# Filling the standing operands of a five-phase product stage: raw halves loaded into the places of their own low parts, instead of through two spare buffers

## The chip, the cores and the metric

One core of one Trainium2 chip runs the kernel. The metric is device microseconds of one execution. The kernel before took 1764.42 us (median of 3 runs, 1763.62 to 1765.13). The profiled execution, from which every duration below comes, took 1766.1 us, of which 1763.9 us lie between its first and its last instruction.

## The reference

One layer of a decoder trunk, in float32, for 2048 positions of width 1024:

```
mod = silu(c) @ w_ada + b_ada;  shift, scale, gate = split(mod, 3)
u = x * (1 + scale) + shift
q, k, v, a_gate, p_in, p_gate, m_a, m_p = split(u @ w_in)
a = sliding_window_sink_attention(q, k, v, sinks, bias, mask) * silu(a_gate)
a = a @ w_attn_proj
p = grouped_linear(multiscale_causal_pool(p_in)) * pool_scale * silu(p_gate)
p = p @ w_pool_proj
y = (sigmoid(m_a) * a + sigmoid(m_p) * p) @ w_out * (1 + gate)
x = layer_norm(2**0.25 * x + y)
```

The change touches the stage of the last three products: `a @ w_attn_proj`, `p @ w_pool_proj` and `y @ w_out`.

## The kernel before

**Products in parts.** A float32 matrix product is done as three products of the rounded type fp32r: every operand is split into a high part (a cast, on ACT) and a low part (operand minus high part, a tensor_tensor on DVE), and `mm3` multiplies high by high, high by low and low by high. Besides, products of 2 x 2 blocks are done with seven block products in place of eight (`front`, `back`), so that for one half of the sequence the standing operand is kept as seven blocks, named B11, T1, T2, B21, T3, B22 and T4. The profile leaves the numbers of names out: its `set_B` is B11, B21 or B22, and its `set_T` is T1 to T4. One *set* is a tile of 128 x 4 x 2 x 512: four pieces of 512 columns, each with a high and a low place beside each other. One *product* below is `product(...)`: one set against one split weight, 4 pieces x 3 = 12 matmuls.

**The last stage** runs in five phases of products: attention projection of sequence half 0, pool projection of half 0, the same two for half 1, and the output projection. The sets are the same tiles in all phases, so between two phases all seven are filled anew. Each phase has groups of two quads (a quad is a 2 x 2 block of the weight), and one group takes 14 products in a fixed order, which the prediction numbers 0 to 13: T2 and B21 of the first quad (0, 1), T2 and B21 of the second (2, 3), T3 and B22 of the first (4, 5), T3 and B22 of the second (6, 7), T4 twice (8, 9), and then, for the next group, B11 and T1 of its first quad (10, 11) and of its second (12, 13). After each product `tick` calls what hooks are due at that position. In the last group of a phase, products 10 to 13 and all that follow need the sets of the next phase; I call the last group of a phase with the first products of the next a *hand-over*. There are four. In three of them (attention to pool, pool to attention, attention to pool) the new sets lie in DRAM unsplit, as two halves of 512 KB each, and `set_steps` loads and splits them; for the fourth (pool to output) they lie there split already and are loaded straight into place by `fill_set`, which the change does not touch.

**What `set_steps` does before.** It takes the 14 halves in the order of PLAN. The raw half goes into a *spare* buffer (`ph.spare()`, 128 x 1024; this pool has two); at its position in SPLIT_AT a cast on ACT writes the high places (profile: `ACT CAST set_B<-spare`, or `set_T`), and a subtraction on DVE the low places (`DVE TENSOR_TENSOR set_B<-spare,set_B`). The first two halves are asked for at position 0, and half k + 2 at the position of the split of half k, whose buffer it takes over.

**What sets the order.** Each engine runs its own queue in order. `sp` issues nearly all loads and stores of this stage, so a load on it waits behind whatever the queue waits for. The other users of the queues in a hand-over are these:

- The weights: `Quad.load` loads a quad into W (two buffers) and A22; POOL forms sums (L294, `sum1`; L298 and L299, `mid`; L303, `late`); `pair_split` casts on ACT (L325) and subtracts on DVE (L132); `half_split` does the same for T4 (L332, L132). PE's products wait for these.
- The gates: each quad gives four results of two halves, and for each of the eight results of a group a 256 KB piece of the gate is loaded (`ga`, L587, in attention phases; `gp`, L597, in pool phases). DVE multiplies the result by it (L590, L598).
- In pool phases POOL adds the gated result to the attention part (L600, `wide`), and `sp` stores the sum three ticks later (`y_d<-wide`, 256 KB).
- DVE also adds partial products in PSUM (L383, L405), and ACT copies them there (L368, L369).

Of the kernel before, what the change touches and what calls it, by code (L numbers as in the profile page):

```python
# [59 lines left out]
def kernel(  # L60
# [23 lines left out]
    pe, act, dve, pool, sp = (Ordered(tc, e) for e in (nc.tensor, nc.scalar, nc.vector, nc.gpsimd, nc.sync))  # L84
# [6 lines left out]
    def set_tile(pl, n):  # L91
        return pl.tile([P, 4, 2, CH], F32R, tag=f"set_{n}", name=f"set_{n}")

    sets = {n: set_tile(cp, n) for n in ("B11", "T1", "B21")}
# [33 lines left out]
    def as32(ap):  # L128
        return ap.bitcast(F32)

    def low(engine, dst, src, hi):
        engine.tensor_tensor(dst, src, as32(hi), ALU.subtract)  # L132
# [53 lines left out]
    def split_set(name, i, src, n=1, eng=None):  # L186
        a, d = eng or (nc.scalar, nc.vector)
        t = sets[name]
        dst = t[:, i : i + n]
        hi, lo = dst[:, :, 0, :], dst[:, :, 1, :]  # L190
        if n == 1:
            hi, lo = t[:, i, 0, :], t[:, i, 1, :]
        a.copy(hi, src)
        low(d, lo, src, hi)
# [6 lines left out]
    def fill_set(name, half, src, eng=None):  # L201

        dst = as32(sets[name][:, 2 * half : 2 * half + 2])
        (eng or nc.sync).dma_start(dst, src[2 * half : 2 * half + 2].rearrange("i p h c -> p i h c"))
# [115 lines left out]
    def by_two(t):  # L320
        return t.rearrange("p (a c) -> p a c", a=2)
# [175 lines left out]
    def steps(hooks, groups, start, todo):  # L497
# [9 lines left out]
    PLAN = (  # L507
        (0, "B11", 0), (1, "B11", 1), (2, "T1", 0), (4, "T1", 1), (5, "T2", 0), (6, "T2", 1), (8, "B21", 0),
        (9, "B21", 1), (11, "T3", 0), (12, "T3", 1), (14, "B22", 0), (15, "B22", 1), (17, "T4", 0), (18, "T4", 1),
    )  # L510

    SPLIT_AT = (1, 2, 3, 4, 6, 7, 11, 12, 13, 14, 15, 16, 17, 18)

    def set_steps(ph, store):


        if store["B11"].shape[0] == 4:
            return [(p, lambda n=n, h=h: fill_set(n, h, store[n])) for p, n, h in PLAN]
        raw, todo = {}, []

        def fetch(k):
            name, half = PLAN[k][1:]
            raw[k] = ph.spare()
            sp.dma_start(raw[k], store[name][half].rearrange("p a b -> p (a b)"))

        def split(k):
            name, half = PLAN[k][1:]
            split_set(name, 2 * half, by_two(raw[k]), 2, (act, dve))

        for k, at in enumerate(SPLIT_AT):  # L530
            if k < 2:
                todo.append((0, lambda k=k: fetch(k)))
            todo.append((at, lambda k=k: split(k)))
            if k + 2 < len(SPLIT_AT):
                todo.append((at, lambda k=k: fetch(k + 2)))
        return todo

    def planned(hooks, ph, store, last, pending={}):
        if last:
            pending["steps"] = set_steps(ph, store)  # L540
        for p, f in pending["steps"]:
            if (p < 14) == last:
                hooks.setdefault((-1, p) if last else (0, p - 14), []).append(f)
        return hooks
# [967 lines left out]
```

## Time and profile before

| | us |
|---|---|
| median of 3 runs | 1764.42 |
| profiled execution | 1766.1 |
| its span, first to last instruction | 1763.9 |
| PE busy (share of the span) | 1702.4 (97%) |
| DVE busy | 1206.9 (68%) |
| ACT busy | 934.1 (53%) |
| POOL busy | 794.2 (45%) |

The five phases of products take the span from about 1283 us to its end. The hand-overs that the change touches begin with their product 0 at 1323.67 (attention to pool, half 0), 1399.83 (pool to attention) and 1511.40 us (attention to pool, half 1). A busy share is an average over the whole span, so the prediction goes by stretches of the span: for a stretch the profile gives the busy time of each engine, the granted clock of PE (1.00 is full) and the share of the DMA engines. A row of waits gives the waiting engine and line, what it waited for, the total in us, how many times, and the longest. A row of a timeline gives start and length in us, the engine, the line, the operation and, in brackets, the idle time ahead of it with what ended it.

### The profile page before, as it was taken

How to read it: one execution, taken by the hardware profiler on the slowest of the kernel's cores; microseconds unless marked ns; L12 is line 12 of the kernel's file. 1: busy time of each engine (PE TensorE's matmuls, PEld its weight loads, DVE VectorE, ACT ScalarE, POOL GpSimd, SP SyncE). 2: the span in 40 equal slices, each digit the busy share in tenths (PEclk: the TensorE clock that was granted, in tenths of full speed). 3: DMA queues.
4: the chain of work that ended last, by engine and by line, in shares of the span. 5: the costliest groups of instructions: out<-in, count | busy, mean ns of one | idle time of the engine just before them, and what ended most of it. 6: DMA issues, size and time to landing. Idle time of an engine off the chain costs nothing. (4 is left out here: it accounts for less than half of the span.)

```text
span 1763.9 us, 24990 instructions
## 1 busy us (share of the span) xinstructions
PE 1702.4 (97%) x8248; PEld 1427.4 (81%) x8248; DVE 1206.9 (68%) x2178; ACT 934.1 (53%) x1973; POOL 794.2 (45%) x618
## 2 busy tenths in 40 slices
PE   6899999999999998999999999999999989999997
PEld 5688888878888887888788888888888867888785
DVE  5977665655777776766655367777867676764777
ACT  4644444545777775544444377777734343423452
POOL 2154444431356567534434125456763562364542
PEclk9999999999999999999999999999999999999998
DMA  9385767844354567787777634544796675789442
GB/s 364 117 289 174 269 208 270 273 145 132 108 174 147 171 217 288 249 288 253 258 264 261 232 96 135 177 159 141 265 349 215 197 256 169 240 302 386 162 143 108
DMA packets 180466, 381.30 MB, mean 216 GB/s; under 512 B 18785, under 2 KB 39281, under 8 KB 180337
## 3 DMA queue, kind: packets, MB, share of 16 engines
q1 hardware_dynamic: 173696, 363.92, 60.5%
q0 software_dynamic: 3552, 11.56, 1.7%
q10 hardware_dynamic: 3088, 4.23, 0.8%
q8 instruction: 65, 1.06, 0.3%
q14 instruction: 65, 0.52, 0.1%
HBM read 244.35 MB, written 138.44 MB: 217 GB/s over the span
## 5 line engine op out<-in xcount | busy, mean ns | idle before, releaser
L56 PE MATMUL mm<-set_B,w_set 128*128 128x512 f32 x3240 | 798.7, 395 | 14.5 <-ACT u L376 6.3
L56 PEld LDWEIGHTS mm<-set_B,w_set 128*128 128x128 f32 x3240 | 603.3, 189 | 142.6 <-DVE w_set L132 10.3
L56 PE MATMUL lg<-set_T,w_set 128*128 128x512 f32 x2088 | 509.1, 394 | 18.4 <-DVE w_set L132 11.0
L56 PEld LDWEIGHTS lg<-set_T,w_set 128*128 128x128 f32 x2088 | 391.4, 189 | 111.0 <-DVE w_set L132 17.9
L132 DVE TENSOR_TENSOR w_set<-W,w_set 128x1024 fp32r<-128x1024 f32 x162 | 227.9, 1407 | 185.8 <-ACT w_set L325 180.8
L325 ACT CAST w_set<-W 128x1024 fp32r<-128x1024 f32 x162 | 169.8, 1049 | 251.6 <-PE mm L56 190.3
L56 PE MATMUL mm<-set_T,w_set 128*128 128x512 f32 x1080 | 265.5, 394 | 0.0
L56 PEld LDWEIGHTS mm<-set_T,w_set 128*128 128x128 f32 x1080 | 200.5, 188 | 41.0
L294 POOL TENSOR_TENSOR W<-W,A 128x512 f32<-128x512 f32 x56 | 82.1, 1466 | 227.6 <-DMA W<-in_win_dram 63.6
L303 POOL TENSOR_TENSOR W<-W 128x512 f32<-128x512 f32 x56 | 80.5, 1438 | 174.5 <-DVE w_set L132 165.2
L56 DVE TENSOR_TENSOR o<-pv,o 64x128 f32<-64x128 f32 x256 | 72.3, 283 | 89.8 <-ACT o L56 86.9
L56 ACT ACTIVATE L<-L,nm 128x257 f32<-128x257 f32 (+1 forms) x256 | 127.1, 498 | 9.3 <-DVE nm L56 3.9
L298 POOL TENSOR_TENSOR W<-W 128x512 f32<-128x512 f32 x56 | 90.5, 1618 | 84.7 <-DVE w_set L132 75.6
L56 DVE CUSTOM_DVE_ANT_0 L<-lg,bt,nsink 128x256 f32<-128x256 f32 (+1 forms) x256 | 111.6, 473 | 5.0 <-PE lg L56 0.8
L299 POOL TENSOR_TENSOR W<-W 128x512 f32<-128x512 f32 x56 | 84.7, 1513 | 37.9 <-DMA W<-in_win_dram 21.9
L56 POOL TENSOR_TENSOR w_set<-W,w_set 128x1024 fp32r<-128x1024 f32 x14 | 33.7, 2404 | 139.6 <-ACT w_set L56 96.9
L56 POOL TENSOR_TENSOR p<-nxt,pg 128x512 f32<-128x512 f32 x32 | 41.7, 1302 | 105.5 <-DVE sm L56 101.8
L56 ACT COPY o<-pv 64x256 f32<-64x256 f32 x128 | 47.3, 370 | 78.0 <-PE pv L56 77.2
L56 DVE TENSOR_TENSOR ptl<-pt,pth 128x512 fp32r<-128x512 f32 (+1 forms) x128 | 85.7, 669 | 1.9 <-ACT pth L56 1.7
L56 PE MATMUL lg<-kk,qs 128*128 128x256 f32 (+1 forms) x512 | 80.5, 279 | 0.0
L56 ACT ACTIVATE L<-L,sm 128x256 f32<-128x256 f32 (+1 forms) x128 | 64.2, 502 | 29.8 <-DVE sm L56 29.8
L56 ACT CAST pth<-pt 128x512 fp32r<-128x512 f32 (+1 forms) x128 | 73.5, 574 | 10.3
(212 smaller groups left out, 2296.3 us busy)
## 6 DMA issues: line engine op xcount, KB each, us to landing
W<-in_win_dram SPq DMA_DIRECT2D x48, 512.0 KB, 5.5
w_set<-wmix_d SPq DMA_DIRECT2D x32, 512.0 KB, 5.4
W<-in_win_dram SPq DMA_DIRECT2D x34, 256.0 KB, 3.7
A<-in_win_dram SPq DMA_DIRECT2D x34, 256.0 KB, 5.1
ag_d<-sig SPq DMA_DIRECT2D x32, 256.0 KB, 3.8
pg_d<-sig SPq DMA_DIRECT2D x32, 256.0 KB, 4.0
ma_d<-sig SPq DMA_DIRECT2D x32, 256.0 KB, 4.0
mp_d<-sig SPq DMA_DIRECT2D x32, 256.0 KB, 4.0
```

The source lines that it names most:

```text
L56: return lambda *args, **kw: self.tc.keep_in_program_order(op(*args, **kw))
L132: engine.tensor_tensor(dst, src, as32(hi), ALU.subtract)
L294: e.tensor_tensor(self.w[:, 1, :], self.w[:, 2, :], self.a22, ALU.add)
L298: e.tensor_tensor(x[:, 1, :], x[:, 1, :], x[:, 0, :], ALU.subtract)
L299: e.tensor_tensor(x[:, 2, :], x[:, 0, :], x[:, 2, :], ALU.subtract)
L303: e.tensor_tensor(x[:, 3, :], x[:, 3, :], x[:, 1, :], ALU.subtract)
L325: a.copy(by_two(hi), raw)
```

## The change

The spare buffers are no longer used here. A raw half (128 x 2 x 512) is loaded into the low places of the two pieces of the set that it will become, ACT casts from there into the high places, and DVE subtracts in place: low place minus high place, into the low place. A set can therefore be loaded only after its last product of the old phase. FETCH_AT names that position for each set, and both halves are asked for there: B11 and T1 at position 0, T2 at 3, B21 at 4, T3 at 7, B22 at 8, T4 at 10. The splits of B11 and T1 move one position later (2, 3, 4, 5 in place of 1, 2, 3, 4); the others keep theirs.

```diff
-    SPLIT_AT = (1, 2, 3, 4, 6, 7, 11, 12, 13, 14, 15, 16, 17, 18)
+    SPLIT_AT = (2, 3, 4, 5, 6, 7, 11, 12, 13, 14, 15, 16, 17, 18)
+
+    FETCH_AT = {"B11": 0, "T1": 0, "T2": 3, "B21": 4, "T3": 7, "B22": 8, "T4": 10}
...
-        raw, todo = {}, []
-
-        def fetch(k):
-            name, half = PLAN[k][1:]
-            raw[k] = ph.spare()
-            sp.dma_start(raw[k], store[name][half].rearrange("p a b -> p (a b)"))
-
-        def split(k):
-            name, half = PLAN[k][1:]
-            split_set(name, 2 * half, by_two(raw[k]), 2, (act, dve))
-
-        for k, at in enumerate(SPLIT_AT):
-            if k < 2:
-                todo.append((0, lambda k=k: fetch(k)))
-            todo.append((at, lambda k=k: split(k)))
-            if k + 2 < len(SPLIT_AT):
-                todo.append((at, lambda k=k: fetch(k + 2)))
-        return todo
+        todo = []
+
+        def raw(name, half):
+            return as32(sets[name][:, 2 * half : 2 * half + 2, 1, :])
+
+        def fetch(name, half):
+            sp.dma_start(raw(name, half), store[name][half])
+
+        def split(name, half):
+            t = sets[name][:, 2 * half : 2 * half + 2]
+            act.copy(t[:, :, 0, :], raw(name, half))
+            low(dve, t[:, :, 1, :], raw(name, half), t[:, :, 0, :])
+
+        for at, (_, name, half) in zip(SPLIT_AT, PLAN):
+            todo.append((FETCH_AT[name], lambda n=name, h=half: fetch(n, h)))
+            todo.append((at, lambda n=name, h=half: split(n, h)))
+        return sorted(todo, key=lambda t: t[0])
```

The first place where this moves instructions is SP's queue in the hand-over from pool to attention. `y_d` is the store of a result, `gp` a gate, `W` a weight; `ain1_B11` and the like are the raw sets in DRAM. Before, two raw halves stand together, and the next two only after them, between stores and weights:

```order
L56 DMA y_d_142<-wide3_13292 128x4x128
L56 DMA spare_13999<-ain1_B11_114 128x1024
L56 DMA spare_14001<-ain1_B11_114 128x1024
L597 DMA gp_14145<-mp_d_141 128x512
L56 DMA spare_14018<-ain1_T1_115 128x1024
L56 DMA spare_14047<-ain1_T1_115 128x1024
L597 DMA gp_14166<-mp_d_141 128x512
L287 DMA W_14091<-in_wap_dram 128x512
L289 DMA W_14091<-in_wap_dram 128x2x512
L56 DMA spare_14064<-ain1_T2_116 128x1024
L56 DMA spare_14088<-ain1_T2_116 128x1024
L56 DMA y_d_142<-wide4_13172 128x4x128
```

Now eight raw halves (B11, T1, T2, B21) stand ahead of the first weight:

```order
L56 DMA y_d_142<-wide3_13292 128x4x128
L598 DMA gp_14125<-mp_d_141 128x512
L56 DMA set_B11_66<-ain1_B11_114 128x2x512 x2
L56 DMA set_T1_67<-ain1_T1_115 128x2x512 x2
L56 DMA set_T2_235<-ain1_T2_116 128x2x512 x2
L56 DMA set_B21_68<-ain1_B21_117 128x2x512 x2
L56 DMA y_d_142<-wide4_13172 128x4x128
L287 DMA W_14071<-in_wap_dram 128x512
L289 DMA W_14071<-in_wap_dram 128x2x512
L56 DMA y_d_142<-wide6_13174 128x4x128
```

The weights of the next group moved behind the raw halves of T2 and B21, and the raw halves moved ahead of the stores that stood between them.

The second place is ACT's queue in the same hand-over, where PE waits for the casts of weights (L325). Before, the cast of the first half of B11 stands ahead of the cast of the second quad's weight (`W_13843`), and each cast of a set reads a spare buffer:

```order
L325 CAST w_set_13982<-W_13799 128x1024
L369 COPY p5_13978<-mm_13918 128x512
L56 CAST set_B11_66<-spare_13999 128x2x512
L368 COPY lg_14025<-mm_13951 128x512
L325 CAST w_set_14028<-W_13843 128x1024
L369 COPY p5_14024<-mm_13952 128x512
L56 CAST set_B11_66<-spare_14001 128x2x512
L325 CAST w_set_14070<-W_13799 128x1024
L56 CAST set_T1_67<-spare_14018 128x2x512
L56 CAST set_T1_67<-spare_14047 128x2x512
L325 CAST w_set_14117<-W_13843 128x1024
```

Now it stands behind it (the second quad's weight is `W_13829` here):

```order
L325 CAST w_set_13968<-W_13785 128x1024
L369 COPY p5_13964<-mm_13904 128x512
L368 COPY lg_14007<-mm_13937 128x512
L325 CAST w_set_14010<-W_13829 128x1024
L369 COPY p5_14006<-mm_13938 128x512
L56 CAST set_B11_66<-set_B11_66 128x2x512 x2
L325 CAST w_set_14050<-W_13785 128x1024
L56 CAST set_T1_67<-set_T1_67 128x2x512 x2
L325 CAST w_set_14099<-W_13829 128x1024
```

One cast of a set moved behind one cast of a weight; the later casts of sets keep their places among the weights.

## The prediction, made before the changed kernel had run

> **What bounds the kernel now.** I read the stretches of the span first, then the waits inside the stretch that loses time, then the timelines. Three stretches of 22 products each (the 14 of a hand-over and the next 8), from the start of product 0:
>
> ```profile
> 1323.67:1383.51 59.84, 59.84 (x266) 49.57 (x265) 47.80 (x48) 27.21 (x31) 22.44 (x14) 1.00 0.64 206
> 1399.83:1473.33 73.50, 64.53 (x266) 49.80 (x265) 56.04 (x48) 28.29 (x33) 36.77 (x22) 0.98 0.72 232
> 1511.40:1571.30 59.90, 59.90 (x265) 49.36 (x264) 41.19 (x38) 23.88 (x28) 33.80 (x21) 1.00 0.72 228
> ```
>
> The columns are length, then busy time of PE, its weight load, DVE, ACT and POOL, granted clock, DMA share, GB/s. The first and third, from attention to pool, run at 59.84 / 22 = 2.72 us a product with PE always busy: PE bounds them, and a faster split brings nothing there. The second, from pool to attention, does the same products in 73.50 us: 73.50 - 59.84 = 13.66 us are lost, and they are all that this change can win. Its waits:
>
> ```profile
> ACT set_T L56 <- DMA spare<-ain_T: 22.2, 8, 5.2
> ACT set_B L56 <- DMA spare<-ain_B: 18.3, 5, 7.3
> ...
> DVE w_set L132 <- ACT w_set L325: 10.5, 2, 8.8
> ...
> PE lg L56 <- DVE w_set L132: 5.6, 6, 1.9
> ...
> SPq L56 <- DVE set_B L56: 12.7, 5, 5.1
> SPq L56 <- POOL wide L600: 11.6, 6, 3.7
> SPq L56 <- DVE set_T L56: 6.4, 3, 2.7
> ```
>
> PE waits for split weights (L132), not for sets. But ACT stands 22.2 + 18.3 = 40.5 us before 13 casts whose raw half hasn't landed, and the casts of weights are queued behind them. SP asks late because it waits for the split that frees a spare buffer (12.7 + 6.4 us) and for POOL's sums (11.6), which its stores need. The chain reads so at the first stall, in the timelines of SP, ACT, DVE and PE:
>
> ```profile
> 1398.32 0.99 SPq L56 DMA_DIRECT2D spare<-ain_B  x2
> 1402.94 1.05 ACT L56 CAST set_B<-spare 128x1024 fp32r<-128x1024 f32 x1 [7.00 <-DMA spare<-ain_B]
> 1404.41 1.04 ACT L325 CAST w_set<-W 128x1024 fp32r<-128x1024 f32 x1
> 1405.49 1.23 DVE L132 TENSOR_TENSOR w_set<-W,w_set 128x1024 fp32r<-128x1024 f32 x1 [8.76 <-ACT w_set L325]
> 1406.77 2.56 PE L56 MATMUL lg<-set_T,w_set 128*128 128x512 f32 x10 [0.53 <-DVE w_set L132]
> ```
>
> The cast of the weight could have been made before 1402.94 but for the cast of B11 ahead of it. The loss by halves of the stretch, and DVE's part up to the first weight of product 14:
>
> ```profile
> 1399.83:1445.11 45.28, 39.99 (x169) 30.94 (x168) 35.28 (x29) 18.08 (x21) 28.89 (x16) 1.00 0.71 224
> 1445.11:1473.33 28.22, 24.54 (x98) 18.86 (x97) 20.75 (x20) 10.21 (x12) 7.88 (x6) 0.94 0.75 245
> 1405.49:1445.73 40.24, 35.01 (x146) 26.81 (x146) 35.90 (x29) 15.54 (x18) 28.36 (x15) 1.00 0.72 222
> ```
>
> Products 0 to 13 lose 45.28 - 14 x 2.72 = 7.20 us, products 14 to 21 lose 28.22 - 8 x 2.72 = 6.46 us.
>
> **The change part by part.** *The splits themselves* stay: 42 casts and 42 subtractions. A cast reading rows 1024 elements apart is already among L325's (the quad's second pair) and they do not differ; an in-place subtraction has a row too:
>
> ```profile
> L325 ACT CAST w_set<-W x47: 1038/1052/1057, 1289.7 to 1598.6; 128x1024 fp32r<-128x1024 f32 x47
> L132 DVE TENSOR_TENSOR w_set<-W,w_set x46: 1207/1226/2311, 1290.8 to 1596.7; 128x1024 fp32r<-128x1024 f32 x46
> L56 DVE TENSOR_TENSOR spare<-spare,cb x8: 1215/1767/2318, 715.7 to 932.3; 128x1024 f32<-128x1024 f32 x8
> ```
>
> 1215 against 1207 ns at the least: 0.01 us each, 0.3 us for 42, off PE's path; taken as nothing. *The loads* stay 512 KB but are written in pieces of 2 KB in place of 4. The nearest rows, weights in 2 KB pieces and ready sets of weights in 4 KB pieces:
>
> ```profile
> W<-in_win_dram SPq DMA_DIRECT2D x48, 512.0 KB, 5.5
> w_set<-wmix_d SPq DMA_DIRECT2D x32, 512.0 KB, 5.4
> ```
>
> 0.1 us of latency each; nothing, where a half is asked for 10 us ahead.
>
> *Earlier loads, pool to attention.* B11 still goes out behind the same store (1398.3), so its halves land at 1403 as now; but the cast of the second quad's weight now stands ahead of it, so the first stall goes. T1 waits for the end of its last product, 1399.83, and lands by about 1407 (raw halves here take 3.1 to 6.9 us, row below). T2 can go at the end of product 2 (1408.0) and is split at position 6, four products or 10.9 us later; B21 at the end of 3 for position 11; T3, B22 and T4 have 13 us and more. Before:
>
> ```profile
> 1412.34 1.05 ACT L56 CAST set_T<-spare 128x1024 fp32r<-128x1024 f32 x1 [4.51 <-DMA spare<-ain_T]
> 1422.22 1.05 ACT L56 CAST set_T<-spare 128x1024 fp32r<-128x1024 f32 x1 [5.17 <-DMA spare<-ain_T]
> 1448.27 1.05 ACT L56 CAST set_T<-spare 128x1024 fp32r<-128x1024 f32 x1 [4.42 <-DMA spare<-ain_T]
> 1466.62 4.15 PE L56 MATMUL lg<-set_T,w_set 128*128 128x512 f32 x10 [1.85 <-DVE w_set L132]
> ...
> DMA to landing us min/median/max: 3.1/4.4/6.9
> ```
>
> In products 14 to 21 POOL is nearly free and DVE has 28.22 - 20.75 = 7.5 us idle, nearly all behind such casts: I take the whole 6.46 us back there. In products 0 to 13 DVE itself comes next. From 1405.49 to 1445.73 it works 35.90 us; one subtraction (1.23) moves ahead, which leaves 34.7. It can begin at 1404.0, when the first raw half is cast, and ends no sooner than 1438.7. Product 14 would start at 1399.83 + 38.08 = 1437.9 and needs its low weight with its third matmul, at 1438.4. So 0.3 us is the least that stays lost, and 7.20 the most. DVE idles 40.24 - 35.90 = 4.3 us there now; half of it is its waiting for products, which stays: 2.2 us. With 0.5 us for restarts of PE I take 0.3 + 2.2 + 0.5 = 3.0 us as still lost. *Sum there: 13.66 - 3.0 = 10.7 us less*, between 6.5 and 13.4.
>
> *New waits, attention to pool.* SP now waits for PE: the next group's weights stand behind B21's load, thus behind the end of product 3. Now:
>
> ```profile
> 1331.94 0.33 SPq L287 DMA_DIRECT2D W<-in_wpp_dram  x1
> 1337.86 1.49 POOL L294 TENSOR_TENSOR W<-W,A 128x512 f32<-128x512 f32 x1 [10.50 <-DMA W<-in_wpp_dram]
> 1345.44 1.06 ACT L325 CAST w_set<-W 128x1024 fp32r<-128x1024 f32 x1 [1.80 <-issue]
> 1350.87 2.88 PE L56 MATMUL mm<-set_B,w_set 128*128 128x512 f32 x12
> ```
>
> Product 3 ends at 1323.67 + 4 x 2.72 = 1334.6; two loads later, at 1335.4, W goes, 3.5 us later than now. T2 and B21 (2 MB, from 1332 on) are ahead of it; at the 345 GB/s that the stretch just before moves (row below) they take 6 us, so W lands near 1341.5 and POOL's sum is done at 1343, in place of 1339.35. The cast of it began at 1345.44: 2.4 us to spare, and product 10 at 1350.87 has about as much again. So nothing, in both such hand-overs; beyond some 4 us more each microsecond costs one. The last two gates also move behind B22 (end of product 7, 1345.4), land near 1351 and delay DVE to 1353; the weight behind them is wanted for product 12 at 1356.3.
>
> ```profile
> 1285.60:1323.70 38.10, 37.85 (x172) 30.90 (x171) 21.53 (x27) 12.31 (x19) 20.23 (x18) 1.00 0.93 345
> ```
>
> In pool to attention W goes at about 1412 in place of 1414.2, no later than now.
>
> **Sum.** The profiled execution should take 1766.1 - 10.7 = 1755.4 us; against the median of the runs, 1764.42 - 10.7 = 1753.7 us.
>
> **The rivals.** *DVE and POOL in each other's way.* The same subtractions take longer where POOL adds; by shape, in the stretch that loses time and in the one that doesn't:
>
> ```profile
> L56 DVE TENSOR_TENSOR set_B<-spare,set_B 128x1024 fp32r<-128x1024 f32 x6 | 10.9, 1837 | 0.3 <-ACT set_B L56 0.2
> ...
> L56 DVE TENSOR_TENSOR set_B<-spare,set_B 128x1024 fp32r<-128x1024 f32 x6 | 9.4, 1573 | 1.6 <-ACT set_B L56 1.6
> ...
> L600 POOL TENSOR_TENSOR wide<-gp,wide 128x512 f32<-128x512 f32 x8 | 16.6, 2085 | 3.5 <-DVE gp L598 3.5
> ```
>
> If the same 28.36 us of POOL meet DVE in fewer us, the idle time that is saved turns into longer subtractions: products 0 to 13 keep their 7.20 us, the gain is 6.46, the time 1758.0. For it: DVE has 0.3 us of slack by the sum above. Against it: the tail doesn't depend on it, and DVE also reads PSUM in that time (L383, L598), at 0.68 us whatever POOL does. The Trainium skill ("SBUF — State Buffer", section "Who interferes with whom") says that a VectorE instruction with two SBUF inputs and a GpSimd instruction that reads SBUF exclude each other for whole instructions. The trace agrees: 1.21 us alone, up to 2.3 beside POOL. By that rule this rival would hold in full, 1758.0.
>
> *Loads no earlier.* B22 and T4 stand behind stores that wait for POOL; if POOL's order, which also changes, makes these late, half of each wait stays and the gain is below 3.5 us: about 1762. Against it: the stores now ahead of T3 are those of the first two sums only.
>
> *Slower: the next group's weights come late.* Both attention-to-pool hand-overs would have to lose more than the gain: (10.7 + 3.5) / 2 = 7.1 us each, so W some 4 + 7 = 11 us later than I reckon, which gives 1768 or more. For it: eight raw halves now stand ahead of W in the queue, and SP waits for PE four times. Against it: 2 MB take 6 us, not 17.
>
> The clock matters for the size: after the last stall it fell.
>
> ```profile
> 1467.00:1468.00 1.00, 1.00 (x4) 0.81 (x3) 0.97 (x2) 0.00 (x0) 1.00 (x1) 0.50 0.39 57
> ```
>
> Those 10 matmuls took 4.15 us in place of 2.56, so 1.6 of the 13.66 us are half clock. If one stall of 2 us stays and does so again, the time is 1755.3. The Trainium skill ("TensorE: Matmul & The Clock Gate", "What's actually happening") has the clock halved only after an idle window of about 3.4 us; here 1.85 us of waiting, in a stretch with other stops, went before it, so the measured row decides.
>
> **How the numbers follow.** My forecast (most of both halves won) has 0.64, the DVE rival 0.18, loads no earlier 0.10, slower 0.08. The predicted time is the forecast's, 1753.7. The range goes from the least loss, 1764.42 - 13.4 = 1751.0, past the DVE rival to 1761; what is left out above is the slower rival and most of the late loads. Runs of this kernel spread by 0.05% to either side of their median, and with another kernel's spread 0.2% (3.5 us) is what can be told from no change. Forecast and DVE rival are faster by more, and so is a little of the rest: 0.84; within 0.2%: 0.10; slower: 0.06.
>
> **What would show it.** In the stretch from product 0 of the pool-to-attention hand-over, 22 products take 60 to 64 us, at full clock. ACT's waits for raw halves there fall from 40.5 us to below 10, and SP's waits for DVE's splits vanish for waits on PE. DVE is nearly never idle up to product 14, and what PE still waits for is L132 near products 10 and 14. The attention-to-pool stretches stay at 59.84. I am wrong if PE waits appear there, if DVE's subtractions go to 2.2 us throughout, or if raw halves of T3 to T4 still hold ACT.

## The result, and the profile after

The changed kernel took 1754.46 us (median of 4 runs, 1753.06 to 1755.00) beside 1764.02 us (4 runs, 1761.71 to 1765.13): ratio 0.9946, 95% interval 0.9929 to 0.9964. It is faster by 9.6 us; the prediction said 1753.7. The profiled execution took 1753.06 us, its span is 1751.3 us.

The three stretches of 22 products after the change, from product 0 of each hand-over (length, then busy time of PE, its weight load, DVE, ACT, POOL, granted clock, DMA share, GB/s):

```profile
1321.40:1381.24 59.84, 59.84 (x266) 49.55 (x264) 52.77 (x48) 27.75 (x32) 23.04 (x15) 1.00 0.64 218
1397.56:1459.13 61.57, 60.64 (x265) 49.32 (x264) 56.74 (x48) 27.66 (x32) 38.38 (x21) 1.00 0.77 263
1475.45:1535.29 59.84, 59.84 (x265) 49.55 (x264) 51.82 (x48) 27.72 (x32) 24.79 (x15) 1.00 0.65 220
```

The two stretches from attention to pool have PE busy from end to end, as before. The one from pool to attention fell from 73.50 to 61.57 us: of the 13.66 us lost, 1.73 are left, and the clock is at 1.00. The ends of the three rows also show that nothing moved between the stretches: product 0 of the second comes 76.16 us after that of the first in both kernels.

A correction to the text ahead of the prediction, and to the prediction's third stretch: the third hand-over begins at 1489.64 us in the trace of before, not at 1511.40, which is its product 8. PE is busy throughout from either start, so no term of the sum changes.

The waits around that stretch (1392.56 to 1471.06), first those of ACT and PE, then SP's own:

```profile
ACT set_B L56 <- DMA set_B<-ain_B: 1.0, 2, 0.8
...
PE lg L56 <- DVE w_set L132: 0.5, 1, 0.5
PE lg L56 <- ACT w_set L325: 0.4, 1, 0.4
```

```profile
SPq L56 <- POOL wide L601: 15.6, 6, 5.0
...
SPq L56 <- PE lg L56: 9.6, 4, 6.2
SPq L56 <- PE mm L56: 4.7, 7, 1.0
```

ACT's 40.5 us behind raw halves became 1.0. SP no longer waits for DVE's splits (19.1 us before); it waits for PE's last product with a set instead (9.6 + 4.7). No wait of PE in this stretch is put down to a load.

What is left stands at product 14. The timeline of DVE, ACT and PE there:

```profile
1429.62 2.31 DVE L56 TENSOR_TENSOR set_B<-set_B 128x1024 fp32r<-128x1024 f32 x1
...
1431.85 2.31 DVE L56 TENSOR_TENSOR set_T<-set_T 128x1024 fp32r<-128x1024 f32 x1
...
1434.08 1.28 DVE L599 TENSOR_TENSOR gp<-lg,gp 128x512 f32<-128x512 f32 x2
1434.85 0.57 ACT L368 COPY lg<-mm 128x512 f32<-128x512 f32 x1 [7.73 <-DVE gp L599]
...
1435.33 1.05 ACT L325 CAST w_set<-W 128x1024 fp32r<-128x1024 f32 x1
...
1436.42 1.22 DVE L132 TENSOR_TENSOR w_set<-W,w_set 128x1024 fp32r<-128x1024 f32 x1 [1.06 <-ACT w_set L325]
1436.44 0.73 PE L56 MATMUL lg<-set_T,w_set 128*128 128x512 f32 x2 [0.41 <-ACT w_set L325]
...
1437.69 2.56 PE L56 MATMUL lg<-set_T,w_set 128*128 128x512 f32 x10 [0.52 <-DVE w_set L132]
```

Read it upwards from the last row. PE waits for the low part of product 14's weight (L132), which waits for its cast (L325). The cast stood behind a copy that waited 7.73 us for DVE's gate product (L599), and that stood behind the subtraction of T3's first half (1431.85, 2.31 us), a set first used by product 18. No load of a raw half is in this chain. What holds PE is a split that isn't due yet, ahead of one that is.

There is a second candidate that ends at the same moment: POOL's sum for weights (L298) also ends at 1435.3, just when the cast begins, and the profile's own chain puts the cast down to it. Experiment 6 below, whose splits stand in another order, tells the two apart. There the same cast begins at 1434.07 us, while that sum ends only at 1435.31; so the cast doesn't need the sum, and the copy ahead of it is what held it. First the sum in the changed kernel, then the cast and the sum in 6:

```profile
1433.04 2.28 POOL L298 TENSOR_TENSOR W<-W 128x512 f32<-128x512 f32 x1
```

```profile
1434.07 1.05 ACT L325 CAST w_set<-W 128x1024 fp32r<-128x1024 f32 x1
...
1434.01 1.30 POOL L298 TENSOR_TENSOR W<-W 128x512 f32<-128x512 f32 x1
```

### The profile page after: what moved, and what is told of

It reads as the page before. It is cut to its first block, busy times and chain, and to the rows that moved or that the text cites. A ratio compares the mean times of both kernels' runs of the same rounds, so it can differ in the third digit from the quotient of the medians.

```text
span 1751.3 us, 24998 instructions
## 1 busy us (share of the span) xinstructions
PE 1697.7 (97%) x8248; PEld 1427.4 (82%) x8248; DVE 1205.2 (69%) x2178; ACT 934.0 (53%) x1973; POOL 798.3 (46%) x618
## 4 chain that ended last, share of the span: by engine, by line
PE 42%; POOL 3%; DVE 2%; DMA 2%; issue 1%; ACT 1%; POOLq 0%; SPq 0%; DVEq 0%; ACTq 0%
PE mm L56 25%; PE lg L56 14%; PE pv L56 2%; PE pt L56 1%; DMA set_T<-ain_T_split 1%; DVE w_set L132 1%; POOL nxt L56 1%; POOL W L298 0%; DVE wide L56 0%; POOL p L56 0%; POOL wide L601 0%; DMA W<-in_wap_dram 0%; POOL rs L56 0%; ACT L L56 0%; POOL a L56 0%
## 5 line engine op out<-in xcount | busy, mean ns | idle before, releaser
L56 PE MATMUL mm<-set_B,w_set 128*128 128x512 f32 x3240 | 799.0, 395 | 12.6 <-ACT u L376 6.3
L132 DVE TENSOR_TENSOR w_set<-W,w_set 128x1024 fp32r<-128x1024 f32 x162 | 224.0, 1383 | 182.7 <-ACT w_set L325 172.1
L325 ACT CAST w_set<-W 128x1024 fp32r<-128x1024 f32 x162 | 170.6, 1053 | 291.1 <-PE mm L56 221.6
L303 POOL TENSOR_TENSOR W<-W 128x512 f32<-128x512 f32 x56 | 83.5, 1492 | 165.5 <-DVE w_set L132 150.3
L298 POOL TENSOR_TENSOR W<-W 128x512 f32<-128x512 f32 x56 | 90.9, 1624 | 78.6 <-DVE w_set L132 68.9
L299 POOL TENSOR_TENSOR W<-W 128x512 f32<-128x512 f32 x56 | 88.6, 1582 | 33.6 <-DMA W<-in_win_dram 26.6
L56 DVE TENSOR_TENSOR k_lo<-spare,k_hi 128x512 fp32r<-128x512 f32 x61 | 60.4, 992 | 28.5 <-ACT k_hi L56 13.4
```

The costliest lines, as they stand in the source:

```text
L56: return lambda *args, **kw: self.tc.keep_in_program_order(op(*args, **kw))
L298: e.tensor_tensor(x[:, 1, :], x[:, 1, :], x[:, 0, :], ALU.subtract)
L299: e.tensor_tensor(x[:, 2, :], x[:, 0, :], x[:, 2, :], ALU.subtract)
L303: e.tensor_tensor(x[:, 3, :], x[:, 3, :], x[:, 1, :], ALU.subtract)
L325: a.copy(by_two(hi), raw)
```

## The experiments

Each ratio is to the kernel before, run on the same chip. *Lost* is the length of the 22 products from pool to attention less 59.84 us, in that kernel's one profiled execution; the medians come from more executions.

| kernel | median us | before us | ratio, 95% | lost |
|---|---|---|---|---|
| changed kernel | 1754.46 | 1764.02 | 0.9946 (0.9929 to 0.9964) | 1.73 |
| changed kernel again | 1757.41 | 1765.48 | 0.9951 (0.9939 to 0.9963) | 1.76 |
| 1 before, new SPLIT_AT | 1761.95 | 1765.23 | 0.9983 (0.9971 to 0.9996) | 7.08 |
| 2 after, old SPLIT_AT | 1757.30 | 1765.23 | 0.9957 (0.9941 to 0.9973) | 4.74 |
| 3 after, asked two halves ahead | 1757.01 | 1765.23 | 0.9945 (0.9930 to 0.9960) | 3.74 |
| 4 new loads in pool to attention only | 1757.27 | 1765.23 | 0.9955 (0.9939 to 0.9970) | 3.54 |
| 5 new loads in attention to pool only | 1764.70 | 1766.56 | 0.9985 (0.9973 to 0.9997) | 10.82 |
| 6 after, T2 and T3 split later | 1754.71 | 1766.56 | 0.9929 (0.9912 to 0.9947) | 0.83 |
| 6 again | 1754.98 | 1765.48 | 0.9936 (0.9924 to 0.9949) | 0.85 |
| 7 after, without POOL's additions | 1754.16 | 1766.56 | 0.9929 (0.9909 to 0.9949) | 0 |
| 8 before, without POOL's additions | 1762.36 | 1766.56 | 0.9975 (0.9963 to 0.9988) | 8.16 |
| 9 as 6, T3's halves apart | 1754.84 | 1765.48 | 0.9938 (0.9925 to 0.9951) | 0 |
| 10 before, with 6's SPLIT_AT | 1759.03 | 1765.48 | 0.9963 (0.9951 to 0.9974) | 5.26 |

**1 and 2: the two parts of the change apart.** The new positions alone on the kernel before, and the new places and loads with the old positions.

```diff
 # 1, on the kernel before
-    SPLIT_AT = (1, 2, 3, 4, 6, 7, 11, 12, 13, 14, 15, 16, 17, 18)
+    SPLIT_AT = (2, 3, 4, 5, 6, 7, 11, 12, 13, 14, 15, 16, 17, 18)
 # 2, on the changed kernel: the reverse
```

> The kernel before with only the new split positions of B11 and T1; the raw halves still go through two spare buffers. Theory A (PE stalls because ACT stands before raw halves that were asked for late, with casts of weights queued behind): only the first stall goes, 10 to 13 of the 13.66 us stay lost in the pool-to-attention stretch, time 1761 to 1764 us. Theory B (what counts is that the splits of B11 and T1 stand one position later in the queues of ACT and DVE): most of the gain is there, 1755 to 1757 us.

> The changed kernel with the old split positions. Theory A: the cast of B11 stands ahead of the second quad's weight again, but its raw half lands at about the same time, so one stall of at most 1.2 us at product 2 comes back: 1754.5 to 1756 us. Theory B: most of the gain is gone, 1762 to 1764 us.

Stretches and ACT's waits of 1 (from attention to pool, then pool to attention), and the stretch and PE's waits of 2:

```profile
1321.53:1383.85 62.32, 60.43 (x266) 49.41 (x264) 49.50 (x47) 28.03 (x32) 23.30 (x14) 1.00 0.63 199
...
1400.17:1467.09 66.92, 61.71 (x266) 49.01 (x264) 54.34 (x48) 28.08 (x32) 34.96 (x21) 1.00 0.74 241
```

```profile
ACT set_T L56 <- DMA spare<-ain_T: 18.5, 8, 4.2
ACT set_B L56 <- DMA spare<-ain_B: 9.3, 5, 6.0
```

```profile
1397.72:1462.30 64.58, 61.40 (x266) 48.96 (x264) 56.66 (x48) 27.35 (x32) 38.58 (x21) 1.00 0.78 251
```

```profile
PE mm L56 <- DVE w_set L132: 2.0, 1, 2.0
PE lg L56 <- DVE w_set L132: 0.7, 2, 0.5
PE lg L56 <- ACT w_set L325: 0.4, 1, 0.4
```

The positions alone take the loss from 13.66 to 7.08 us, the new places alone to 4.74, both to 1.73. The two parts overlap: alone they save 6.6 and 8.9 in the traces, together 11.9. The medians have 3.3 for 1 and 7.9 for 2 beside 8.1 and 9.6 for both, so 1 is worth less than its trace says; part of that is the 2.48 us that it lost in the stretch before. In 1 the first half of the stretch loses 1.70 us in place of 7.20. So the first stalls came from the casts of B11 and T1 standing ahead of weights while their raw halves were late; that it takes both is shown by 2, where those casts stand ahead again and the loads are early: its products 0 to 9 have no wait of PE above 0.2 us. In 1 ACT still waits 27.8 us for raw halves, and its other 5.38 us of loss lie at products 14 to 21. In 2 the only stall above a microsecond is product 10's (2.02 us). My expectations missed twice here: I had 10 to 13 us still lost in 1, and in 2 at most 1.2 us more, at product 2, and 1756 us at the most.

**3: the same places, but asked no earlier than before.** In place, two halves ahead.

```diff
+        asked = (0, 0) + SPLIT_AT[:-2]
-        for at, (_, name, half) in zip(SPLIT_AT, PLAN):
-            todo.append((FETCH_AT[name], lambda n=name, h=half: fetch(n, h)))
+        for ask, at, (_, name, half) in zip(asked, SPLIT_AT, PLAN):
+            todo.append((max(ask, FETCH_AT[name]), lambda n=name, h=half: fetch(n, h)))
```

> The changed kernel, in place, but each half is asked for at the position of the split two halves earlier, as before. The loads no longer wait for a spare buffer, but stand later in SP's queue, behind stores that wait for POOL. Theory A in its full form (the time of the ask counts): ACT's waits for raw halves come back in part, 10 to 25 of the 40.5 us, 3 to 8 us are lost in the stretch, 1756 to 1761 us. If only the wait for a spare buffer made the loads late: ACT's waits stay below 5 us and the time at 1754 to 1755.5 us.

```profile
1402.70:1466.28 63.58, 61.05 (x266) 49.26 (x265) 54.70 (x48) 27.62 (x32) 35.57 (x21) 1.00 0.78 259
```

```profile
ACT set_T L56 <- DMA set_T<-ain_T: 14.7, 3, 10.4
ACT set_B L56 <- DMA set_B<-ain_B: 3.4, 3, 1.7
```

ACT waits 18.1 us again, the trace has 2.0 us more of loss than the changed kernel's, most of it in one stall of product 10 (1.53 us), and the time did not tell it from the changed kernel. Run 4 below, which asks early, waits 4.1 us and loses 3.54. So ACT's waits for raw halves are not a price by themselves, and asking earlier than two halves ahead has no gain that these runs can tell. What counts is whether something that is due stands behind the wait at that moment.

**4 and 5: one kind of hand-over at a time.** `set_steps` takes the old way (two spare buffers, old positions) in the other kind.

```diff
+        if not (store is ain_d[1]):        # 4;  5: if not (store is not ain_d[1])
...
+            for k, at in enumerate(OLD_SPLIT_AT):
...
+            return todo
```

> The new scheme only in the hand-over from pool to attention; the two from attention to pool go through spare buffers as before. Theory A: the whole gain is there, 1754.5 us within 1.5, about 2 us lost in that stretch. If the other two hand-overs also gained something that their full PE doesn't show: 1757 us or more.

> The new loads in the two attention-to-pool hand-overs alone; pool to attention goes through two spare buffers as before. Theory A (PE is full in those hand-overs, so the new loads bring nothing there): ratio 0.999 to 1.001, the 13.7 us of pool to attention are lost as before, about 7 in its products 0 to 13 and about 6 at products 14 to 21. Rival B (spare buffers lose about 2 us at products 14 to 21 after the first of these hand-overs in some executions, as the two kernels that kept them there showed with 2.48 and 1.36 us lost per 14 products): about 2 us won, ratio 0.9985 to 0.999. Rival C (the next group's weights come late behind the eight raw halves): PE waits for L132 at products 10 to 12 there, slower by 1 us or more.

The first stretch and the pool-to-attention stretch, of 4 and of 5:

```profile
1323.15:1384.86 61.71, 60.87 (x266) 49.18 (x264) 47.41 (x47) 27.07 (x31) 22.30 (x14) 1.00 0.60 198
1401.18:1464.56 63.38, 60.70 (x265) 49.33 (x264) 54.70 (x48) 27.59 (x32) 40.48 (x23) 1.00 0.83 269
```

```profile
1326.07:1385.91 59.84, 59.84 (x265) 49.55 (x264) 52.18 (x48) 27.66 (x32) 23.20 (x14) 1.00 0.67 216
1402.23:1472.89 70.66, 63.88 (x265) 50.08 (x264) 53.97 (x48) 28.48 (x33) 35.63 (x21) 0.98 0.71 230
```

Nearly the whole gain belongs to pool to attention: with the new loads there alone the ratio is 0.9955, where the changed kernel has 0.9946 and 0.9951. My expectation for 4 was about 2 us lost and 1756 us at the most; it was missed on both, the time in part because the kernel before took 1.2 us more on this chip (1765.23 against 1764.02). In 4 the first stretch, on its spare buffers, lost 1.87 us (61.71 - 59.84), and in 1 it lost 2.48 (62.32 - 59.84); in the profiled executions of before, 8 and 10 it lost at most 0.1. So the old way costs a microsecond or two there in some executions. That fits the 0.9985 of 5, but its interval reaches almost to 1, and whether the new loads are worth something in those hand-overs is not settled.

4 and 5 show something else. In 5 the pool-to-attention code is that of before, and it lost 10.82 us where the profile of before shows 13.66: the loss that the prediction took as a fixed price varies by 3 us between profiled executions of the same hand-over code, and the prediction had the dearer one. In 4 this code is that of the changed kernel, and it lost 3.54 us where the changed kernel's two profiles show 1.73 and 1.76. B11's halves went out 0.2 us before product 0 (1400.99 against 1401.18), ACT waited 3.1 us for the first, DVE's first subtraction began 5.75 us after product 0 in place of 3.40, and product 10 waited for its weight, whose subtraction stood behind that of T2's second half. The rows of ACT and PE in 4:

```profile
1405.84 1.05 ACT L56 CAST set_B<-set_B 128x1024 fp32r<-128x1024 f32 x1 [3.08 <-DMA set_B<-ain_B]
...
1430.71 2.56 PE L56 MATMUL mm<-set_B,w_set 128*128 128x512 f32 x10 [1.72 <-DVE w_set L132]
```

So differences of 2 to 3 us between single traces in the column *lost* are no more than what the same code varies by, unless a row shows the stall that went.

**6, 9 and 10: only the order of the splits.** 6 moves T2's second half behind the weight of product 10, and T3's first half behind that of product 14; 9 also puts T3's halves apart; 10 is 6's order on the kernel before.

```diff
-    SPLIT_AT = (2, 3, 4, 5, 6, 7, 11, 12, 13, 14, 15, 16, 17, 18)
+    SPLIT_AT = (2, 3, 4, 5, 6, 10, 11, 12, 14, 14, 15, 16, 17, 18)   # 6, and 10 on the kernel before
+    SPLIT_AT = (2, 3, 4, 5, 6, 10, 11, 12, 14, 15, 16, 17, 18, 19)   # 9
```

> The changed kernel with two splits moved behind weights: the second half of T2 from position 7 to 10, the first half of T3 from 13 to 14 (B21's halves one position up). Theory A (what is left lost is only the order in DVE's and ACT's queues: a split that isn't due stands ahead of the weight of product 10 or 14): the stalls at products 10 and 14 of the pool-to-attention hand-over go, at most 0.5 us of 1.7 stays lost, ratio to the kernel before 0.993 to 0.994. Rival B (DVE has no time left there, beside POOL): as much is lost at other products, 1.5 to 3 us, ratio 0.9946 or worse.

> The version with T2's second and T3's first half split behind the weights of products 10 and 14, once more. If the 0.8 us less of loss in its first trace is real, its ratio is 0.0005 below the changed kernel's of the same chip, 0.9 us, which the intervals will hardly tell apart; a difference of 3 us (0.9929 against 0.9946) would have to show in the trace outside the hand-over, and I expect none there.

> The same with T3's halves at 14 and 15, and all later halves one position later (T4 at 18 and 19), so that the weight of product 16 stands ahead of T3's second half on DVE. Theory A (order alone): the last stall (0.51 us at product 16) goes too, 0 to 0.2 us lost in 22 products, ratio 0.0005 below the version before it. Rival B (DVE full): T3 or B22 is late at product 18 or 19 instead, 0.5 us or more lost there.

> The kernel before (two spare buffers) with the later splits of that version. Theory A (the wait for spare buffers makes the loss, and later splits free them later still): ACT waits 25 us or more for raw halves in the pool-to-attention hand-over, 7 us or more lost, ratio 0.996 to 1.002. Rival B (the order of splits and weights on ACT and DVE would have done without the new places): 3 us or less lost, ratio 0.995 or below.

> The changed kernel itself once more, beside the two versions below, to compare them on one chip. Ratio 0.9946 give or take 0.001; in its pool-to-attention hand-over 1 to 2 us lost in 22 products.

The pool-to-attention stretch of 6 and PE's one stall in it, then the stretch of 9, then that of 10 with the waits of ACT and PE:

```profile
1398.52:1459.19 60.67, 60.16 (x266) 49.49 (x264) 56.43 (x48) 27.50 (x32) 38.07 (x20) 1.00 0.78 262
```

```profile
1443.17 2.58 PE L56 MATMUL lg<-set_T,w_set 128*128 128x512 f32 x10 [0.51 <-DVE w_set L132]
```

```profile
1402.01:1461.85 59.84, 59.84 (x265) 49.56 (x264) 55.31 (x46) 27.60 (x32) 39.63 (x21) 1.00 0.80 270
```

```profile
1401.47:1466.57 65.10, 61.80 (x265) 49.04 (x264) 51.25 (x48) 28.17 (x32) 37.27 (x21) 1.00 0.80 252
```

```profile
ACT set_B L56 <- DMA spare<-ain_B: 14.0, 6, 7.7
ACT set_T L56 <- DMA spare<-ain_T: 13.6, 7, 4.5
...
PE lg L56 <- DVE w_set L132: 2.3, 3, 0.8
PE mm L56 <- DVE w_set L132: 0.9, 1, 0.9
```

6 loses nothing up to product 13 and stalls once, at product 16, by 0.51 us; the other 0.3 of its 0.83 us have no row of their own; I had expected 0.5 us at the most. 9 removes that stall too: 59.84 us, PE busy throughout, with POOL working 39.63 us and DVE 55.31 in the same stretch. In this execution, then, DVE's and POOL's work fit beside PE without loss, and the stalls of 1.73 us that the change leaves come from the order. By time, 9 and 6 are 2.4 to 2.6 us below the changed kernel on the same chip (1754.84 and 1754.98 against 1757.41), but the intervals overlap, and 9 is not below 6; the traces say 1.8 and 0.9. That 9 is faster than the changed kernel is not shown; its one trace is the only one with all of POOL's work and no loss in any of the three hand-overs.

10 was a surprise against my theory of the spare buffers. With both spare buffers kept, ACT still waits 27.6 us for raw halves as that theory has it, yet only 5.26 us are lost where it asked for 7 or more, and the time falls by 0.37%, two thirds to three quarters of what the change brings (0.54% and, on the same chip, 0.49%). Nor was the rival met (3 us or less, 0.995 or below): the order alone gets most of the way, the places the rest.

**7 and 8: POOL's part.** POOL's additions are left out in the last group of the first pool phase, the one ahead of the hand-over from pool to attention. (The expectations say both pool phases; the condition `s == 0` holds for sequence half 0 alone, and 24 of the 32 additions remain in the traces.)

```diff
-            nc.vector.tensor_tensor(g, src, g, ALU.mult)
...
-            nc.gpsimd.tensor_tensor(dst, g, dst, ALU.add)
+            if s == 0 and m >= 4:
+                nc.vector.tensor_tensor(dst, src, g, ALU.mult)
+            else:
+                nc.vector.tensor_tensor(g, src, g, ALU.mult)
+                nc.gpsimd.tensor_tensor(dst, g, dst, ALU.add)
```

> The changed kernel; in the last group of both pool phases POOL's additions are left out, and with them the attention part of those sums: DVE's product goes straight into the buffer that is stored. Theory A (POOL's additions lengthen DVE's subtractions, and that is the rest of the loss): the subtractions of sets in products 0 to 13 of pool to attention take 1.2 to 1.4 us instead of up to 2.3, at most 0.5 us stays lost in the 22 products, ratio to the kernel before about 0.9935. Rival B (the order in the queues alone): 1.5 us or more stays lost though the subtractions are short, ratio 0.9946.

> The kernel before with the same omission (POOL's additions left out in the last group of both pool phases). Theory A (the loss comes from raw halves that are asked for only when a split has freed a spare buffer): ACT still waits 25 us or more for raw halves and 8 us or more of the 13.7 stays lost, ratio 0.997 or above. Rival B (the loss comes from POOL: its late sums hold the stores ahead of the loads in SP's queue, and its additions lengthen the splits): at most 4 us stays lost, ratio 0.9945 or below.

The stretch of 7 and, by shape, DVE's subtractions of sets in its products 0 to 13; then the stretch and ACT's waits of 8:

```profile
1403.06:1462.90 59.84, 59.84 (x266) 49.56 (x264) 52.44 (x48) 27.72 (x32) 20.97 (x13) 1.00 0.82 274
```

```profile
L56 DVE TENSOR_TENSOR set_T<-set_T 128x1024 fp32r<-128x1024 f32 x6 | 10.5, 1753 | 0.2 <-ACT set_T L56 0.2
...
L56 DVE TENSOR_TENSOR set_B<-set_B 128x1024 fp32r<-128x1024 f32 x4 | 5.0, 1256 | 1.1 <-ACT set_B L56 1.1
```

```profile
1399.32:1467.32 68.00, 61.63 (x266) 49.02 (x264) 49.39 (x48) 28.40 (x33) 19.72 (x14) 1.00 0.76 245
```

```profile
ACT set_T L56 <- DMA spare<-ain_T: 19.5, 8, 4.6
ACT set_B L56 <- DMA spare<-ain_B: 15.5, 5, 7.9
```

Without POOL's additions the rest of the loss goes (7), as it does by order alone (9): in these two traces either is enough. The subtractions of `set_B` fell to 1.26 us; those of `set_T` stay at 1.75 in the mean, the long ones beside POOL's sums for weights, so my expectation of 1.2 to 1.4 us was missed for them. On the kernel before (8) the omission leaves ACT 35.0 us behind raw halves and 8.16 us of loss, 2.7 to 5.5 less than in the two executions with the additions; by the medians it is worth 4.2 us. POOL is the smaller part; the queue ahead of the weights is the larger.

## Why the prediction was right, point by point

- **All that can be won is the 13.66 us of pool to attention**: right in that nearly all of the gain is there. But 13.66 is one execution's loss; the same code lost 10.82 in another. The trace gives 11.93 won in this stretch, the timed runs 9.6 and, again, 8.1 us between medians. The working, made against one trace, had 10.7: a loss taken at its dear end and a rest taken too large are errors of opposite sign, and they partly cancelled, and that the sum came within a microsecond is in part luck. With 5's 10.82 us as the loss and 1.73 to 3.54 as the rest (the changed kernel, and 4), 7.3 to 9.1 us are won.
- **3.0 us still lost there**: 1.73. The terms were wrong in kind. The 0.3 us that DVE's work was to cost at the least is not a bound: in 9 DVE does the same work beside the same additions and nothing is lost. It rested on DVE beginning 4.2 us after product 0, and on T3's first half being split before product 14's weight. DVE's first subtraction of a set began 3.40 us after product 0, because B11 went out 3.4 us ahead of product 0 in place of 1.5 (1394.16 against 1397.56); in 4, where it went out only 0.2 us ahead, 3.54 us were lost. And T3's split need not be done before product 14 at all. DVE was not "nearly never idle" either: up to the end of product 13 it idled 3.4 us (38.46 - 35.09). The 2.2 us for idle time that stays and the 0.5 us for restarts had no row of their own.

```profile
1397.56:1436.02 38.46, 38.46 (x169) 31.27 (x167) 35.09 (x28) 16.86 (x19) 26.23 (x14) 1.00 0.82 285
1436.02:1459.13 23.11, 22.18 (x97) 18.05 (x97) 21.65 (x20) 10.81 (x14) 12.16 (x8) 1.00 0.70 228
```

- **Products 14 to 21 fully won**: not quite; 0.93 of 6.46 stayed. Counted to the start of product 14, as in the prediction, 0.80 us are lost ahead of it and 0.93 behind it. But 0.57 of the 0.80 is product 14's own wait for its first matmul (0.41 us idle), so that product costs 1.50 of the 1.73 us, by the stall shown above, and products 0 to 13 cost 0.23. The two rows above cut at the end of product 13's last matmul and so have 0.38 and 1.35. The prediction named the place (L132 near product 14) and left it out of this half's sum.
- **ACT's waits are why weights are late**: right as a chain at the first stall (1), too simple as a price. 40.5 us of waits held 13.66 us of loss, 27.6 us held 5.26 (10), 18.1 held 3.74 (3), and 4.1 held 3.54 (4). The change did two things, and the prediction gave the gain to earlier loads; the position of the splits, which it counted only for B11's first cast, alone won 6.6 us in this stretch as the change has it (1) and 8.4 in the order of 10 (3.7 and 5.6 if 5's 10.82 us is the loss).
- **New waits from attention to pool cost nothing**: right. W went 11.46 us after product 0 in place of 8.27, 3.2 us later where 3.5 were reckoned, and PE did not wait. SP's rows there:

```profile
1330.89 1.88 SPq L56 DMA_DIRECT2D set_B<-pin_B  x2
1332.86 0.55 SPq L287 DMA_DIRECT2D W<-in_wpp_dram  x1
```

- **The rivals.** DVE against POOL: single subtractions are as long as that rival has it (2.31 us at 1429.62 and 1431.85), but the nine of sets up to product 14 took 16.6 us where the nine of before took 16.1, so the saved idle time did not turn into longer ones, and 0.80 us were lost there, not 7.20. The Trainium skill's rule on instructions that exclude each other ("SBUF — State Buffer", "Who interferes with whom") agrees with these durations, 1.21 and 2.31 us. The 1758.0 us that the prediction drew from it does not follow, because the long subtractions had room. Loads no earlier: fell, 1.0 us of waits. Slower: fell, no PE wait in either attention-to-pool stretch.
- **The clock**: 1.6 us of the loss were half clock after the last stall; with stalls of at most 0.52 us it stayed at 1.00. The length of one stall is not what decides it: in 1, after a wait of 3.10 us, the ten matmuls at 1461.97 took 2.56 us, and in before those after the longest wait, 2.02 us, took 2.58. What halves the clock is not shown here.

The spans differ by 12.6 us: 11.93 in this hand-over and 2.27 ahead of the first hand-over, less 1.8 in the output phase (159.8 us from product 14 of its hand-over to the end before, 161.6 after), with 0.2 in between. The change reaches neither the first stage nor the output phase; I take those differences as variation between executions, and no run singles them out.

## What to carry to other kernels

A wait on an in-order queue costs only what stands behind it and is due: before giving loads more room, look at what a waiting cast or subtraction holds up, and put each split behind the weights that are needed sooner. Here a table of 14 numbers won some two thirds of the gain without the new places, and with them another one left nothing of the last 1.7 us in its trace, though the medians can't confirm it. Take a loss from more than one execution before it becomes the price in a sum: this one read 13.66 and 10.82 us for the same code before the change, and 1.73, 1.76 and 3.54 for the same code after it.

## What the hardware showed that was not expected

Loading a half in place costs SP more than loading it into a spare buffer. The durations of one issue (min, median, max in ns), in the changed kernel and in the kernel before, for the same 512 KB:

```profile
L56 SPq DMA_DIRECT2D set_T<-pin_T x16: 518/518/526, 1320.0 to 1502.6; - x16
...
DMA to landing us min/median/max: 3.6/5.5/12.6
```

```profile
L56 SPq DMA_DIRECT2D spare<-pin_T x16: 319/319/328, 1328.5 to 1535.4; - x16
```

The prediction priced the pieces of 2 KB by their latency alone (0.1 us) and took them as nothing. Each issue takes 0.2 us more of SP, 42 x 0.2 = 8.4 us over the three hand-overs. From issue to landing the loads of T1 to T4 took 5.5 us in the median where the spare buffers' took 4.2 in the same part of the span; whether the pieces or the fuller queue did that is not shown. No wait of PE in the changed kernel's three hand-overs is put down to one of these loads.
